# Queries and keys of layer 1's third head from seven products of quarters, in a two-layer hybrid step

## The chip, the core and the metric

The kernel runs on one core of one Trainium2 chip, in one launch. The metric is the device time of an execution in microseconds (us), lower is better; the time of a version is the median of its runs. One further execution is taken with the hardware profiler; all rows of the profile come from that one.

## The reference

Two layers over 640 token rows: one prompt of 512 rows and eight running streams of 16 rows each. Layer 0 is stick-breaking attention with 16 heads, layer 1 is gated linear attention (GLA) with 4 heads. What matters here is layer 1, cut to:

```python
q, k, v, r, a_lr = jnp.split(h @ w_in, [nk, 2 * nk, 2 * nk + nv, 2 * nk + 2 * nv], axis=-1)
# 4 heads: q and k 256 columns each, v and r 512 columns each; h has 2048 columns
g = log_sigmoid(a_lr @ w_a2 + b_a) / GLA_TAU           # the decays
S_t = diag(exp(g_t)) S_{t-1} + k_t^T v_t;  o_t = q_t S_t   # per head, in chunks
o = rmsnorm(o) * g_out
y = (o * silu(r)) @ w_out
```

The prompt starts from a zero state; each stream starts from its own state of 4 x 256 x 512 numbers, which is read and written once. All is float32 in and out.

## The kernel before

**Precision.** A float32 product is made of three matmuls in the type that TensorE runs at full rate: each operand is split into a high and a low half (`halves`, L134 on ScalarE and L135 on VectorE), and high x high, high x low and low x high are added up in PSUM.

**Two ways to project.** The activations of a layer are kept in quarters (`Quarters`: two halves of the 2048 columns, two halves of the 640 rows). `by_sevens` takes a job of 256 output columns and computes it with seven products of quarters in place of eight; the sums of quarters of the activations are ready (`sums`), those of the weights are made on VectorE for each job (L507 to L513). A product is 8 x 3 = 24 matmuls of 320 columns, a job 168 of them, all at L541. `plain` takes a part of 128 output columns and computes it directly: 2 x 2 x 8 x 3 = 96 matmuls of 320 columns at L596; two parts, 192 matmuls, stand for one job.

**Stages of layer 1.** First `six` and one call of `plain` make the first head's values and queries. Then a list `jobs` goes through `by_sevens` (L1352 to L1355), 17 jobs: keys of head 0, queries and keys of head 1, the values of heads 1 to 3 and the gates of all heads. Here nothing else is woven in but the short transposes that the values need. Then comes **the heads' stage** (from L1395 on), the GLA recurrence itself. Its PSUM banks are shared out anew, and its work is cut into lanes, each a generator:

- `decays` makes the decays of each head and scales its queries and keys;
- `prompt_lane` goes through 16 units (4 heads of 4 chunks of 128 rows). Each unit carries the state `S` on: scores, products with the state's two halves (`S1h`, `S1l`: one buffer each, L1582 and L1583), the update of `S` (L1646, L1648), then norm and transposes (L1470, L1474, L1492) and a store of the result `og`;
- `sample_lane` goes through 16 groups of 4 stream states. Per group: four matmuls at L1754 read four state tiles `s`, then four matmuls at L1760 and four operations at L1762 update them, and GpSimd's queue stores them and loads the next ones into the same buffers (7 buffers for 64 tiles). After a head's fourth group come norm, transposes and the store of its `og`;
- `fetches` reads the rows of `og` back, splits them and so prepares the output projection.

**Fillers.** The lanes are short instructions with waits between them. Between their steps, `drive` puts the long rows of matmuls that depend on no lane: first `others` (L1414), the plain products for queries and keys of heads 2 and 3 (8 parts, 768 matmuls at L596), and after them two calls of `share` (g = 0 and 1: 240 matmuls of 512 columns each at L642), which multiply the finished `og` rows of heads 0 and 1 by the output weights. `share` for g = 0 can start when both lanes are through head 0 and the rows of `og` are back; for g = 1 when head 1 is through. What is left of the output projection (L360 and L1894) follows when all lanes have ended.

**What sets the order.** TensorE's instructions are written in a fixed order, which it keeps: a step that isn't ready holds up all behind it. The place of each lane step is chosen at build time by a class `Side`: a clock `pe["now"]` is advanced by a cost per matmul that is issued, a lane says after how much of that clock its next step is due, and `tick` issues the steps that are due between two pieces of filler. Where no filler is left, the clock just goes on and the lane steps stand directly behind one another. The other engines' order is made by the tool's scheduler. The table `came` connects the filler with the lanes: `came["of"]` is the last head whose queries and keys have been made by `keep` (L1397), and `decays` does not start head 2 or 3 before that; `came["plain"]` and `came["last"]` let `fetches` use the buffers that the plain products share with it.

Of the kernel before, what the change touches and what calls it, by code (L numbers as in the profile page):

```python
# [15 lines left out]
P = 128  # L16
# [11 lines left out]
NK = 1024  # L28
# [13 lines left out]
def hybrid_step_kernel(ctx: ExitStack, tc: tile.TileContext, A: dict, O: list):  # L42
# [7 lines left out]
    pe = {"now": 0.0, "quad": 4800}  # L50
# [3 lines left out]
    def by(l, r):  # L54

        n = r.free_size()
        if l.dtype == F32R:
            pe["now"] += n / 2400 + 0.0133
        elif l.free_size() <= 32:
            pe["now"] += n / pe["quad"] + 0.01  # L60
        else:
            pe["now"] += n / 600 + 0.005
        return r
# [9 lines left out]
    def store(out, in_):  # L73
        nc.sync.dma_start(out=out, in_=in_)
# [24 lines left out]
    def bank(tag):  # L99
        return psum["pool"].tile([P, 512], F32, tag=tag, name=f"ps_{tag}", bufs=psum["bufs"][tag])  # L100
# [22 lines left out]
    gq_d, gk_d = ([dp.tile([P, 2, T], F32, name=f"{n}_{h}") for h in range(GH)] for n in ("gq", "gk"))  # L123
# [25 lines left out]
    def wraw(src, a, n):  # L149
        r = wp.tile([P, 1024], F32, tag="wr", name="wr", bufs=WR)[:, :a * n]  # L150
        load(r.rearrange("p (a n) -> p a n", a=a), src)
        return r

    def wsplit(r, a):
        return [t.rearrange("p (a n) -> p a n", a=a) for t in split(r)]
# [422 lines left out]
    def plain(h, src, parts, upper=None):  # L578

        todo = [(n0, k0, leave) for n0, leave in parts for k0 in (8, 0)]  # L580

        def piece(n):
            if n < len(todo):
                n0, k0, _ = todo[n]
                return wraw(src[:, k0 // 8:k0 // 8 + 15:2, n0:n0 + P], 8, P)

        nxt, raw, acc = wsplit(piece(0), 8), piece(1), None
        for n, (n0, k0, leave) in enumerate(todo):
            wh, wl = nxt
            if k0:  # L590
                acc = [bank("mm")[:, :HALF] for _ in hs]
            for nt in range(2):
                for k in range(8):
                    hi, lo = h.part(k0 + k, nt)
                    for l, r, first, last in ((wh, hi, True, False), (wh, lo, False, False), (wl, hi, False, True)):
                        mm(acc[nt], l[:, k, :], by(l[:, k, :], r), start=k0 == 8 and k == 0 and first,  # L596
                           stop=k0 == 0 and k == 7 and last)
                    if k % 2:
                        yield
                if nt == 0 and raw is not None:  # L600
                    nxt, raw = wsplit(raw, 8), piece(n + 2)
                if k0 == 0:
                    leave(nt, acc[nt])
            if upper is not None and n == len(todo) - 2:
                upper()

    def keep_in(d):
        def f(out):
            for hh in range(2):
                store(d[:, hh, :], out[hh])  # L610
        return f
# [77 lines left out]
    h1, h2 = Quarters(), Quarters()  # L689
# [8 lines left out]
    with tc.tile_pool(name="st", bufs=1, reuse_waits="tile") as st:  # L698
# [50 lines left out]
        def ring(tags):  # L749
            n = 0  # L750
            while True:
                tag = tags[n % len(tags)]
                yield ad_ring() if tag is None else sp.tile([P, 1024], F32, tag=tag, name="ar")
                n += 1
# [3 lines left out]
        last = ring(["s14", "s15", None, None])  # L758
# [38 lines left out]
    with tc.tile_pool(name="wq", bufs=1, reuse_waits="tile") as wq:  # L797
# [22 lines left out]
        def keep_value(p):  # L820
            return lambda out: side.add(rows0(out, p, v_d[p], vp_rows, vs_rows))

        jobs = []
# [328 lines left out]
    src = w_in1.rearrange("(kt p) n -> p kt n", p=P)  # L1152
    s1_pool = ExitStack()
    sp = s1_pool.enter_context(tc.tile_pool(name="sp1", bufs=1, reuse_waits="tile"))
    with tc.tile_pool(name="o0", bufs=1, reuse_waits="tile") as po, ExitStack() as only_d:
# [193 lines left out]
                    store(gr_d[h][:, kt, :], out[s])  # L1349
            return leave  # L1350

        jobs = [(NK, keep_in(gk_d[0])), (256, keep_in(gq_d[1])), (NK + 256, keep_in(gk_d[1]))]  # L1352
        jobs += [(2 * NK + 512 * h + 256 * n, keep_value(h, n)) for h in range(1, GH) for n in range(2)]
        jobs += [(2 * NK + D + 512 * h + 256 * n, keep_gate(h, n)) for h in range(GH) for n in range(2)]
        sevens = by_sevens(h2, w_in1, wq, jobs)  # L1355
# [37 lines left out]
        return w_out1.rearrange("(kt p) n -> p kt n", p=P)[:, k0:k0 + 2, 512 * c:512 * c + 512]  # L1393

    with tc.tile_pool(name="gl", bufs=1, reuse_waits="tile") as gl:  # L1395
        came = {"plain": False, "last": False, "of": 1, "when": 0.0}

        def keep(dst, hh):
            t = []

            def leave(nt, pt):
                if nt == 0:
                    t.append(gl.tile([P, T], F32, tag="pl", name="pl", bufs=2))
                    came["last"] = dst is gk_d[3] and hh == 1
                nc.scalar.copy(t[0][:, hs[nt]], pt)
                if nt:
                    nc.scalar.dma_start(out=dst[:, hh, :], in_=t[0])
                    for h in (2, 3):
                        if hh and dst is gk_d[h]:
                            came.update(of=h, when=pe["now"])  # L1410
            return leave


        others = plain(h2, src, [(n0 + P * hh, keep(dst, hh)) for h in (2, 3)  # L1414
                                 for n0, dst in ((256 * h, gq_d[h]), (NK + 256 * h, gk_d[h])) for hh in range(2)],
                       lambda: came.update(plain=True))
        for _ in range(2):
            next(others)
# [69 lines left out]
        def leave(h, t0, on, g):  # L1488

            tp = bank("tp")  # L1490
            for s in range(4):
                turn_block(tp[:, P * s:P * s + P], block(on[:, P * s:P * s + P]), ident)  # L1492
            dve.tensor_tensor(g, tp.rearrange("p (s t) -> p s t", s=4), g, op=ALU.mult)
            move(og_d[h][:, :, t0:t0 + P], g)
# [332 lines left out]
    with tc.tile_pool(name="o1", bufs=1, reuse_waits="tile") as po:  # L1827
# [54 lines left out]
        for i in range(4):  # L1882
            r = wraw(w_of(2 + i // 2, 3, i % 2), 2, 512)
            h, lo = (po.tile([P, 1024], F32R, name=f"{n}{i}") for n in ("kh", "kl"))
# [3 lines left out]
        for a in range(TOK):  # L1888
            acc = bank("mm")
            for n in range(8):  # L1890
                wh, wl = kept[n // 2]
                h, lo = (x[:, P * a:P * a + P] for x in og1[8 + n])
# [30 lines left out]
```

## Time and profile before

| what | before |
|---|---|
| median of 3 runs | 2579.01 us (2577.28 to 2580.81) |
| the profiled execution's own time | 2576.39 us |
| its span, first to last instruction | 2574.6 us |
| mean clock granted to TensorE | 0.979 of full speed |
| TensorE busy | 2444.2 us, 95% of the span |
| VectorE, ScalarE, GpSimd busy | 1604.6, 1019.7 and 231.4 us |
| moved by DMA | 502.05 MB, mean 195 GB/s |

The span is the distance between the first and the last instruction that the profiler saw; the execution's own time lies 1.8 us above it. The busy time of TensorE counts matmuls that overlap once. In the views below, rows of a timeline begin with start and length in us; an idle time in brackets is that of the engine just before the row, with what ended it. In a view by windows, each row is a stretch of the span, with the busy time of TensorE (PE), its weight loads (PEld), VectorE (DVE), ScalarE (ACT) and GpSimd (POOL) in it, the number of instructions in brackets, the granted clock (1.00 is full speed), the share of the 16 DMA engines in use and what they moved.

### The profile page before, as it was taken

How to read it: one execution, taken by the hardware profiler on the slowest of the kernel's cores; microseconds unless marked ns; L12 is line 12 of the kernel's file. 1: busy time of each engine (PE TensorE's matmuls, PEld its weight loads, DVE VectorE, ACT ScalarE, POOL GpSimd, SP SyncE). 2: the span in 40 equal slices, each digit the busy share in tenths (PEclk: the TensorE clock that was granted, in tenths of full speed). 3: DMA queues.
4: the chain of work that ended last, by engine and by line, in shares of the span. 5: the costliest groups of instructions: out<-in, count | busy, mean ns of one | idle time of the engine just before them, and what ended most of it. 6: DMA issues, size and time to landing. Idle time of an engine off the chain costs nothing. (4 is left out here: it accounts for less than half of the span.)

```text
span 2574.6 us, 43617 instructions
## 1 busy us (share of the span) xinstructions
PE 2444.2 (95%) x17321; PEld 2147.2 (83%) x17321; DVE 1604.6 (62%) x2445; ACT 1019.7 (40%) x1820; POOL 231.4 (9%) x489
## 2 busy tenths in 40 slices
PE   6899999999999999999999979899999998989998
PEld 4589999989999988787777758899999997766776
DVE  4675655555566656666776665766666655666466
ACT  4342222222223335655443344333333364565133
POOL 1220000000000000000000050000000114334200
PEclk8899999999999999999999989999999999999999
DMA  9966666766663366666665853344444367777464
GB/s 337 320 212 218 217 204 219 228 216 192 207 199 118 116 209 207 228 213 222 214 226 170 252 188 123 88 114 130 126 124 118 112 221 249 240 250 230 164 230 148
DMA packets 452797, 502.05 MB, mean 195 GB/s; under 512 B 26090, under 2 KB 349810, under 8 KB 452466
## 3 DMA queue, kind: packets, MB, share of 16 engines
q1 hardware_dynamic: 433090, 442.11, 54.1%
q0 software_dynamic: 16048, 51.92, 6.0%
q10 hardware_dynamic: 3456, 5.24, 0.6%
q8 instruction: 136, 2.23, 0.4%
q14 instruction: 67, 0.55, 0.1%
HBM read 410.05 MB, written 89.13 MB: 194 GB/s over the span
## 5 line engine op out<-in xcount | busy, mean ns | idle before, releaser
L541 PE MATMUL ps_mm<-sums,wh 128*128 128x320 f32 x2880 | 644.0, 312 | 2.2 <-ACT wh L134 2.2
L541 PEld LDWEIGHTS ps_mm<-sums,wh 128*128 128x128 f32 x2880 | 481.2, 189 | 11.3 <-issue 7.4
L541 PE MATMUL ps_mm<-h,wh 128*128 128x320 f32 x2160 | 484.7, 312 | 5.7 <-DVE u L547 3.2
L541 PE MATMUL ps_mm<-sums,wl 128*128 128x320 f32 x1440 | 446.4, 310 | 1.5 <-DVE wl L135 1.5
L541 PEld LDWEIGHTS ps_mm<-h,wh 128*128 128x128 f32 x2160 | 360.3, 188 | 22.1 <-issue 14.5
L135 DVE TENSOR_TENSOR wl<-wr,wh 128x1024 fp32r<-128x1024 f32 x192 | 236.0, 1230 | 213.9 <-ACT wh L134 213.1
L134 ACT CAST wh<-wb 128x1024 fp32r<-128x1024 f32 x178 | 186.8, 1049 | 449.6 <-PE ps_mm L541 381.6
L541 PE MATMUL ps_mm<-h,wl 128*128 128x320 f32 x1080 | 334.5, 310 | 0.7 <-DVE wl L135 0.7
L134 ACT CAST wh<-wr 128x1024 fp32r<-128x1024 f32 x192 | 201.6, 1050 | 316.0 <-PE ps_mm L541 194.1
L541 PEld LDWEIGHTS ps_mm<-sums,wl 128*128 128x128 f32 x1440 | 271.6, 189 | 2.0 <-DVE wl L135 2.0
L135 DVE TENSOR_TENSOR wl<-wb,wh 128x1024 fp32r<-128x1024 f32 x178 | 217.6, 1222 | 63.0 <-ACT wh L134 62.5
L642 PE MATMUL ps_mm<-wh,ogh 128*128 128x512 f32 x460 | 201.8, 439 | 13.2 <-ACT ogh L134 7.5
L596 PE MATMUL ps_mm<-h,wh 128*128 128x320 f32 x896 | 208.0, 319 | 6.1 <-ACT wh L134 3.3
L541 PEld LDWEIGHTS ps_mm<-h,wl 128*128 128x128 f32 x1080 | 203.5, 188 | 1.0 <-DVE wl L135 1.0
L642 PE MATMUL ps_mm<-wh,ogl 128*128 128x512 f32 x460 | 182.8, 397 | 0.6 <-DVE ogl L135 0.4
L642 PE MATMUL ps_mm<-wl,ogh 128*128 128x512 f32 x460 | 182.1, 396 | 0.0
L596 PEld LDWEIGHTS ps_mm<-h,wh 128*128 128x128 f32 x896 | 151.1, 191 | 17.6 <-issue 7.0
L596 PE MATMUL ps_mm<-h,wl 128*128 128x320 f32 x448 | 139.9, 312 | 3.1 <-DVE wl L135 3.1
L642 PEld LDWEIGHTS ps_mm<-wh,ogh 128*128 128x128 f32 x460 | 87.9, 191 | 41.5 <-issue 14.8
L898 DVE TENSOR_TENSOR_SCAN k<-k,zero_c 128x544 f32<-128x544 f32 (+4 forms) x96 | 93.3, 976 | 29.6 <-ACT k L894 16.9
L470 PE MATMUL ps_mm<-wh,h 128*128 128x512 f32 x288 | 101.7, 418 | 6.8 <-ACT h L134 4.9
L642 PEld LDWEIGHTS ps_mm<-wh,ogl 128*128 128x128 f32 x460 | 87.4, 190 | 21.8 <-DVE ogl L135 1.8
(341 smaller groups left out, 3830.6 us busy)
## 6 DMA issues: line engine op xcount, KB each, us to landing
ar<-in_w_ada_dram SPq DMA_DIRECT2D x160, 512.0 KB
wb<-in_sb_w_in_dram SPq DMA_DIRECT2D x82, 512.0 KB
kc<-in_cache_sb_k_dram SPq DMA_DIRECT2D x64, 512.0 KB
vc<-in_cache_sb_v_dram SPq DMA_DIRECT2D x64, 512.0 KB
wb<-in_gla_w_in_dram SPq DMA_DIRECT2D x51, 512.0 KB
wr<-in_gla_w_in_dram SPq DMA_DIRECT2D x45, 512.0 KB
wr<-in_sb_w_in_dram SPq DMA_DIRECT2D x44, 512.0 KB
ar<-in_w_ada_dram SPq DMA_DIRECT2D x64, 256.0 KB
```

Of the source, the lines that this page charges most:

```text
L134: nc.scalar.copy(hi, x)
L135: dve.tensor_tensor(lo, x, hi.bitcast(F32), op=ALU.subtract)
L470: mm(acc[a], l, by(l, r[:, e, :]), start=j == 0 and e == 0 and first, stop=j == 7 and e == 1 and last)
L541: mm(acc, l[:, k, :], by(l[:, k, :], r), start=start and k == 0 and first, stop=k == 7 and last, skip_group_check=True)
L596: mm(acc[nt], l[:, k, :], by(l[:, k, :], r), start=k0 == 8 and k == 0 and first, stop=k0 == 0 and k == 7 and last)
L642: mm(acc, l, by(l, r[:, e, :]), start=i == 0 and e == 0 and first, stop=i == 1 and e == 1 and last)
L898: dve.tensor_tensor_scan(kr, kr, zeros[:, :w], 1.0, ALU.mult, ALU.add)
```

## The change

The queries and keys of head 2 (the third) become two more jobs of `by_sevens`, behind those of head 1 and ahead of the values, and their four parts leave the plain products of the heads' stage. The list has 19 jobs then, and `others` has 4 parts (384 matmuls). `came["of"]` starts at 2, since head 2's queries and keys are there when the stage begins.

```diff
-        jobs = [(NK, keep_in(gk_d[0])), (256, keep_in(gq_d[1])), (NK + 256, keep_in(gk_d[1]))]
+        jobs = [(NK, keep_in(gk_d[0]))]
+        jobs += [(n0 + 256 * h, keep_in(d[h])) for h in (1, 2) for n0, d in ((0, gq_d), (NK, gk_d))]
...
-        came = {"plain": False, "last": False, "of": 1, "when": 0.0}
+        came = {"plain": False, "last": False, "of": 2, "when": 0.0}
...
-                    for h in (2, 3):
-                        if hh and dst is gk_d[h]:
-                            came.update(of=h, when=pe["now"])
+                    if hh and dst is gk_d[3]:
+                        came.update(of=3, when=pe["now"])
...
-        others = plain(h2, src, [(n0 + P * hh, keep(dst, hh)) for h in (2, 3)
-                                 for n0, dst in ((256 * h, gq_d[h]), (NK + 256 * h, gk_d[h])) for hh in range(2)],
+        others = plain(h2, src, [(n0 + P * hh, keep(dst, hh)) for n0, dst in ((256 * 3, gq_d[3]), (NK + 256 * 3, gk_d[3]))
+                                 for hh in range(2)],
                        lambda: came.update(plain=True))
```

With half the filler, the places of the lanes' steps on TensorE move. Two places show it.

The first is TensorE in the heads' stage, behind the last group of head 0's stream states (`s` in L1754 is a state tile, `qz` the queries, `krh` and `krl` the halves of the prompt's keys, `aTh` and `aTl` those of its scores, `on` a normed result that is transposed). Before:

```order
L596 MATMUL ps_mm<-h,wh 128x320 x2
L596 MATMUL ps_mm<-h,wl 128x320
L1445 MATMUL ps_tp<-v,aTh 128x512 x2
L1445 MATMUL ps_tp<-v,aTl 128x512
L1760 MATMUL ps_tp<-vst,kst_21143 128x512
```

The change, from the last state of the same group on:

```order
L1754 MATMUL ps_z<-s_22618,qz_21591 32x512
L1492 MATMUL ps_tp<-ident,on 128x128 x4
L1760 MATMUL ps_tp<-vst,kst_21593 128x512
L1445 MATMUL ps_tp<-v,krh 128x512 x2
L1445 MATMUL ps_tp<-v,krl 128x512
L1760 MATMUL ps_tp<-vst,kst_21593 128x512 x3
L1457 MATMUL ps_tp<-q,k 128x128 x2
L1605 MATMUL ps_tp<-ident,k 128x128 x2
L1445 MATMUL ps_tp<-v,aTh 128x512 x2
```

The rows of L596 between the lanes' steps are gone; in the change none stands from shortly behind the third group of head 0 on, and the first row of L642 comes only when head 0 is through both lanes and its rows are back.

The second place is the end of the stage, TensorE around the last group of stream states (head 3), with the last `share` (L642) and the first rows of the final projection (L360). Before:

```order
L1754 MATMUL ps_z<-s_24695,qz_21141 32x512
L1754 MATMUL ps_z<-s_24761,qz_21141 32x512
L642 MATMUL ps_mm<-wh,ogh 128x512
L642 MATMUL ps_mm<-wl,ogh 128x512
L642 MATMUL ps_mm<-wh,ogl 128x512
L1760 MATMUL ps_tp<-vst,kst_21143 128x512
```

The change:

```order
L1754 MATMUL ps_z<-s_24762,qz_21590 32x512
L1760 MATMUL ps_tp<-vst,kst_21592 128x512 x4
L1754 MATMUL ps_z<-s_24764,qz_21591 32x512
L1754 MATMUL ps_z<-s_24766,qz_21591 32x512
L1754 MATMUL ps_z<-s_24768,qz_21591 32x512
L1754 MATMUL ps_z<-s_24788,qz_21591 32x512
L1760 MATMUL ps_tp<-vst,kst_21593 128x512 x4
L1492 MATMUL ps_tp<-ident,on 128x128 x4
L360 MATMUL ps_mm<-wh,ogh 128x512
```

Before, 13 triples of L642 stand between the last two groups and 5 behind the last one; in the change the last `share` has ended ahead of them, and the lanes' steps follow one another.

## The prediction

> **What bounds the kernel now.** The page first, for who is busy:
>
> ```profile
> span 2574.6 us, 43617 instructions
> ...
> PE 2444.2 (95%) x17321; PEld 2147.2 (83%) x17321; DVE 1604.6 (62%) x2445; ACT 1019.7 (40%) x1820; POOL 231.4 (9%) x489
> ```
>
> TensorE is busy 95% of the span, so a matmul less should be time less. That average hides two different stages, so I then read the chain that ended last, in order of time (start, us, what):
>
> ```profile
> 1878.81 179.76 PE ps_mm L541 x1224
> ...
> 2305.13 5.05 DMA og_in<-og
> ...
> 2322.85 6.28 PE ps_mm L642 x27
> ...
> 2461.00 75.74 PE ps_mm L360 x328
> ```
>
> In the seven-products stage the chain is one solid run of L541: 179.76 / 1224 = 0.147 us per matmul, a job of 168 is 24.7 us. L642 goes at 6.28 / 27 = 0.233 us. Between them the chain hops from engine to engine. A busy window of the first stage:
>
> ```profile
> 1650.00:1675.40 25.40, 25.40 (x176) 25.40 (x175) 15.96 (x17) 8.76 (x10) 0.00 (x0) 1.00 0.40 109
> ```
>
> About one job: PE never idle at full clock, VectorE busy 16.0 of 25.4 us, ScalarE 8.8, DMA at 40%. TensorE is the bound there, and nothing else is near it.
>
> The heads' stage I read by its state groups. PE's timeline gives where it begins, the groups of L1754, the first L642 and the end:
>
> ```profile
> 2059.23 0.53 PE L596 MATMUL ps_mm<-h,wh 128*128 128x320 f32 x2 [0.68 <-DVE out L547]
> ...
> 2119.44 1.07 PE L1754 MATMUL ps_z<-s,qz 128*32 128x512 f32 x8
> ...
> 2133.98 1.06 PE L1754 MATMUL ps_z<-s,qz 128*32 128x512 f32 x8
> ...
> 2171.45 1.92 PE L1754 MATMUL ps_z<-s,qz 128*32 128x512 f32 x2 [6.54 <-DMA s<-in_state_gla_dram]
> ...
> 2259.98 0.48 PE L642 MATMUL ps_mm<-wh,ogh 128*128 128x512 f32 x1
> ...
> 2265.82 0.50 PE L642 MATMUL ps_mm<-wh,ogh 128*128 128x512 f32 x1 [2.85 <-ACT ogh L134]
> ...
> 2269.86 0.80 PE L642 MATMUL ps_mm<-wh,ogh 128*128 128x512 f32 x1 [2.39 <-ACT ogh L134]
> ...
> 2443.77 1.07 PE L1754 MATMUL ps_z<-s,qz 128*32 128x512 f32 x8
> ...
> 2452.03 0.50 PE L360 MATMUL ps_mm<-wh,ogh 128*128 128x512 f32 x1 [2.22 <-DVE gate L1493]
> ```
>
> I cut the stage, 2059.2 to 2452.0, at group starts: the first group of head 0; its third; its fourth; the first and fourth of head 1, of head 2, of head 3; the end.
>
> ```profile
> 2059.20:2119.40 60.20, 58.00 (x383) 56.02 (x383) 32.54 (x62) 37.95 (x72) 8.73 (x17) 1.00 0.71 227
> 2119.40:2151.60 32.20, 31.63 (x193) 26.82 (x192) 27.91 (x51) 22.70 (x44) 10.85 (x19) 1.00 0.78 253
> 2151.60:2163.90 12.30, 12.30 (x88) 11.09 (x90) 7.03 (x14) 4.38 (x9) 5.75 (x10) 1.00 0.85 287
> 2163.90:2223.00 59.10, 48.73 (x263) 41.74 (x262) 28.81 (x53) 30.90 (x60) 19.41 (x32) 0.88 0.69 206
> 2223.00:2276.50 53.50, 45.03 (x248) 35.27 (x247) 32.72 (x61) 25.00 (x51) 20.71 (x34) 0.94 0.83 285
> 2276.50:2317.90 41.40, 37.31 (x177) 28.33 (x176) 25.22 (x41) 29.00 (x52) 15.14 (x25) 1.00 0.71 221
> 2317.90:2360.50 42.60, 42.60 (x214) 32.49 (x214) 29.11 (x55) 25.00 (x50) 16.13 (x29) 1.00 0.66 221
> 2360.50:2404.10 43.60, 36.85 (x151) 28.02 (x150) 21.64 (x36) 13.64 (x26) 14.82 (x25) 0.88 0.64 199
> 2404.10:2443.80 39.70, 39.10 (x183) 28.62 (x183) 20.25 (x28) 4.03 (x5) 11.41 (x21) 1.00 0.54 179
> 2443.80:2452.00 8.20, 6.01 (x32) 4.11 (x31) 5.83 (x10) 3.37 (x5) 2.78 (x5) 1.00 0.37 121
> sum 392.80, PE 357.57 PEld 292.51 DVE 231.06 ACT 195.97 POOL 125.72; mean PE 35.76 PEld 29.25 DVE 23.11 ACT 19.60 POOL 12.57
> ```
>
> PE is idle 35 us of the 392.8, and its clock drops to 0.88 where it waits, although 768 + 480 matmuls of filler lie between the lanes' steps. So the lanes already hold TensorE up here; filler hides their waits and is not simply work in the way. That is the point of the whole forecast.
>
> **The change part by part.**
>
> *The two jobs added.* 2 x 168 = 336 matmuls at L541 by 0.147: **+49.4 us**, all on the path, since that stage is solid PE. Each job's weight sums, splits and evacuations hide under PE, by the window above; without that cover they'd be 16 us of VectorE each. The four stores go out on SP like those of the jobs before, at 40% DMA. Bounds: 49.3 to 51, the upper end for a short wait per job.
>
> *The four parts removed.* 384 matmuls at L596 by 0.147 = 56.4 us of PE work, with eight weight loads of 512 KB, eight splits, eight evacuations and four stores. If PE had nothing else to wait for, this would all come back, and 56.4 - 49.4 = 7 us would be gained. How much of it comes back is the question, and depends on what the lanes need with less filler. Their fixed costs:
>
> ```profile
> out_dram<-s POOLq DMA_DIRECT2D x64, 256.0 KB, 3.6
> s<-in_state_gla_dram POOLq DMA_DIRECT2D x62, 256.0 KB, 4.8
> ...
> og<-gate POOLq DMA_DIRECT2D x20, 256.0 KB, 3.9
> ```
>
> ```profile
> L1762 DVE SCALAR_TENSOR_TENSOR s<-s,es,ps_tp 128x512 f32<-128x512 f32 x64 | 46.7, 743 | 19.1 <-PE ps_tp L1760 18.4 <-DMA s<-in_state_gla_dram 0.2
> ...
> L78 POOL DMA_DIRECT2D out_dram<-s x64 | 35.2, 551 | 96.8 <-DVE s L1762 63.5 <-DVE on_ms L232 26.6 <-issue 2.3
> ...
> L1583 DVE SCALAR_TENSOR_TENSOR S1l<-S,e,S1h 128x512 fp32r<-128x512 f32 x24 | 17.9, 747 | 15.4 <-ACT S1h L1582 15.3
> ...
> L1582 ACT ACTIVATE S1h<-S,e 128x512 fp32r<-128x512 f32 x24 | 17.3, 720 | 17.2 <-PE ps_tp L1445 17.1
> ...
> L1474 ACT ACTIVATE on<-ps_tp,on_r 128x512 f32<-128x512 f32 x16 | 11.0, 686 | 15.4 <-POOL on_r L234 15.4
> ...
> L135 DVE TENSOR_TENSOR ogl<-og_in,ogh 128x640 fp32r<-128x640 f32 x10 | 8.1, 822 | 11.4 <-ACT ogh L134 11.4
> ```
>
> A state cycle, from one group to the next that needs its buffers: L1754 1.1, L1760 0.4, L1762 0.74, store 0.55 + 3.6, load 0.55 + 4.8 (GpSimd's 551 ns to issue, then the time to landing): 11.8 us. With 7 buffers, the fourth state of each group waits for the group before. By stretch, with the rows of filler counted in the order before and after:
>
> - To the first group of head 0: the same 330 matmuls ahead, 60.2, no gain.
> - To the third group: 54 matmuls fewer, 7.9 us of work. From the second group to the third it took 2151.6 - 2134.0 = 17.6 us; the cycle allows 12 to 14: I take **-4**.
> - Third to fourth group: no filler left. Before, the fourth state landed 2171.45 - 2151.6 = 19.9 us on; the cycle alone is 12, with four updates and GpSimd's queue behind them 14: **-6**.
> - Fourth group of head 0 to the first of head 1: before, 2171.45 to 2223.0, 51.6 us, with 156 matmuls of filler; in the change only 12 of L642, at the end. PE work falls to 19 us, and the chain sets the time: norm and transposes of head 0 about 5 (the last stretch's 8.2 us less its 15 rows of L642, 3.5), held up by two units of the prompt lane that stand ahead, each 2 x (0.72 + 0.75 + 0.7) = 4.3 us for the two halves of its state, its `og` out 0.7 + 3.9, its rows back 5.05 and split in two operations of 0.8; sum 25. Then `share` waits once more for the second pair of rows, before 2269.86 - 2259.98 = 9.9 us. Together 35 to 36: **-15.5**.
> - To the fourth group of head 1: 114 matmuls of L596 go and 84 more of L642 come (+2.8 us of work), while the wait for rows of the `share` (2.85 + 2.39 and a slow clock behind it, out of 8.5 us idle in this stretch) has moved ahead; I let 8 us go: **-5.5**.
> - Two stretches through head 2: 96 rows of L642 in place of 108 in each, work -2.8 each, of which the lanes' chain keeps a part: **-4** together.
> - On to head 3: 108 rows in place of 90, 4.2 us of work, half of it in idle time that is there already (6.8 us): **+2**.
> - Head 3's groups: 63 in place of 138, work -17.3; three state cycles of 11.8 are the floor, 35 of 39.7: **-5**.
> - The end: 15 rows of L642 go behind the last group, but norm, gate and transposes still stand ahead of L360: **-0.5**.
>
> Sum -38.5. Against it stands the clock:
>
> ```profile
> 2170.00:2175.00 5.00, 3.54 (x8) 1.88 (x9) 0.20 (x1) 0.00 (x0) 1.07 (x2) 0.50 0.55 202
> ...
> 2180.00:2190.00 10.00, 10.00 (x65) 9.38 (x64) 5.64 (x10) 5.68 (x12) 6.70 (x12) 1.00 0.75 193
> ...
> 2266.00:2272.00 6.00, 3.48 (x8) 2.00 (x9) 1.65 (x3) 1.86 (x3) 3.02 (x5) 0.54 1.00 381
> ```
>
> Behind the wait of 6.54 us the granted clock is 0.50, ten us later 1.00 again; behind two waits of 2 to 3 us it is 0.54. In the change the piece without filler (some 40 us, PE busy less than half) and the last groups would run so, and the first matmuls behind each. Some 8 us of matmuls at half clock that lie on the chain cost 4 us more: **+4**. Bounds 0 and 8.
>
> The Trainium skill, "TensorE: Matmul & The Clock Gate", section "HAM oscillation — how this bites in real kernels", says that a TensorE idle for over about 3.4 us falls back to half its clock and needs as long of sustained work to get it back. It speaks against this change, which takes filler from a stage with waits. The row of 0.50 agrees. By that page, four such restarts at half of 3.4 us each are an estimate of 7 us where I took 4, and the total would come out 3 us later.
>
> So the heads' stage shrinks by 38.5 - 4 = 34.5 us, and the kernel gets 49.4 - 34.5 = **15 us slower**. `decays` for head 2 loses its wait for `came["of"]`; it is then held only until both lanes are through head 0, which came later anyway.
>
> Against the profiled execution (2576.39, span 2574.6, 1.8 around it) this is 2591.4. The median of the runs shown, 2579.01, is 2.6 above that execution; the forecast for the median is 2579 + 15 = **2594**.
>
> **The rivals.**
>
> *The lanes have slack, and TensorE's work alone counts.* Then the filler's 56.4 us come back in full, the jobs cost 49.4, and the time is 2579 - 7 = 2572. For it: 357.6 of 392.8 us busy, and stretches such as 2317.9 to 2360.5 without any idle. Against: after the fourth group of head 0 there is nothing to put in place of the filler; for PE to stay full, the rows of `og` would have to be back 19 us after that group, and the chain above has 25 ahead of its first product. It decides if the stage without filler lasts under 20 us. This is the rival on the faster side.
>
> *The lanes set the pace throughout.* Then only the stretches up to head 0's fourth group (-10) and the last groups (-5) give anything, and the stretch between head 0 and head 1 takes as long as before: -15, so +34, 2613. For it: the stretch to head 3 takes 43.6 us with 36.9 busy, that to head 1 59.1 with 48.7, each with many short waits for ScalarE, VectorE and GpSimd. Against: the last group's end went through in 8.2 us although 15 rows of L642 lay in it, so the lanes can be quick where they must.
>
> *It comes out even.* Gain and cost within 0.2%, 5 us, which is about what a measurement of this kernel can tell from no change. It needs 10 to 20 us more than the 34.5 allowed, so an `og` that is back 10 us sooner than the chain says.
>
> That the change doesn't do what it says I rule out: the order shows both sides, 336 matmuls more and 384 fewer.
>
> **How the numbers follow.** Forecast (+5 to +25) 0.50, time 2594. Lanes at their own pace (+25 to +40) 0.18. Even 0.15. PE alone (-5 and below) 0.17. So slower 0.68, same 0.15, faster 0.17. Eight in ten: below, the rival at 2572 with 3 us for waits of before that may go; above, the rival at 2613 with 3 more of the clock's bound: 2569 to 2616.
>
> **What would show it.** Right: the heads' stage begins 49 us later; its first L642 comes near 128 us after that instead of 200.8 (2259.98 - 2059.23), with much idle PE and a clock under 0.8 in the 40 us before it; the last two groups about 10 us apart with little PE work; the heads' stage near 358 us. Wrong: a stage of 336 us with PE as busy as before (then the lanes had slack), or one of 376 and more, with PE waiting at every head.

## The result, and the profile after

| what | before | after |
|---|---|---|
| median of 4 runs | 2578.15 us (2576.88 to 2580.81) | 2606.56 us (2601.06 to 2609.93) |
| ratio to before | 1 | 1.0107, 95% interval 1.0093 to 1.0121 |
| span of the profiled execution | 2574.6 us | 2604.4 us |
| mean clock granted | 0.979 | 0.973 |

The change makes the kernel 28.4 us slower. The forecast was 15 slower. (One execution of a version further down, of 8353 us, is left out of its ratio.) The page of the changed kernel answers to the first lines shown of before:

```profile
span 2604.4 us, 43543 instructions
...
PE 2451.6 (94%) x17273; PEld 2147.8 (82%) x17273; DVE 1626.0 (62%) x2469; ACT 1025.4 (39%) x1822; POOL 229.3 (9%) x489
```

TensorE has 48 matmuls fewer and 7.4 us more busy time, in a span that is 29.8 us longer. That says that something has come to stand idle, not where. The timeline of TensorE after the change gives the marks by which the heads' stage is cut (start, length, instruction, and in brackets the idle time ahead of it with what ended it):

```profile
2110.51 0.53 PE L596 MATMUL ps_mm<-h,wh 128*128 128x320 f32 x2 [0.68 <-DVE out L547]
...
2174.76 1.06 PE L1754 MATMUL ps_z<-s,qz 128*32 128x512 f32 x8
...
2220.04 1.91 PE L1754 MATMUL ps_z<-s,qz 128*32 128x512 f32 x2 [6.93 <-DMA s<-in_state_gla_dram]
...
2246.65 0.73 PE L642 MATMUL ps_mm<-wh,ogh 128*128 128x512 f32 x1
...
2256.47 0.79 PE L642 MATMUL ps_mm<-wh,ogh 128*128 128x512 f32 x1 [6.07 <-ACT ogh L134]
...
2328.84 1.12 PE L1492 MATMUL ps_tp<-ident,on 128*128 128x128 f32 x4 [6.69 <-ACT on L1474]
...
2367.51 0.80 PE L1457 MATMUL ps_tp<-q,k 128*128 128x128 f32 x2 [4.68 <-DVE k L1555]
...
2460.66 0.40 PE L642 MATMUL ps_mm<-wh,ogl 128*128 128x512 f32 x1
...
2473.66 1.92 PE L1754 MATMUL ps_z<-s,qz 128*32 128x512 f32 x2 [2.88 <-DMA s<-in_state_gla_dram]
...
2481.29 0.80 PE L360 MATMUL ps_mm<-wh,ogh 128*128 128x512 f32 x1 [0.79 <-DVE gate L1493]
```

The stage begins at 2110.5 and no longer at 2059.2: the two jobs cost 51.3 us. It lasts 370.8 us and no longer 392.8: 22.0 came back. What follows it takes 123.1 us in place of 122.6. So 51.3 - 22.0 + 0.5 = 29.8, the whole difference of the spans.

Where those 22.0 come from is read from one view, the busy time by windows, with the stage cut in two at its first L642. Before:

```profile
2059.20:2260.00 200.80, 184.56 (x1130) 163.12 (x1130) 121.33 (x224) 113.80 (x220) 58.95 (x102) 0.97 0.75 240
2260.00:2452.00 192.00, 173.01 (x782) 129.40 (x779) 109.73 (x185) 82.16 (x149) 66.78 (x114) 0.96 0.65 208
```

After:

```profile
2110.50:2246.60 136.10, 111.23 (x632) 91.67 (x633) 88.45 (x167) 85.02 (x167) 41.55 (x73) 0.94 0.76 247
2246.60:2481.30 234.70, 199.78 (x895) 145.82 (x893) 135.67 (x236) 100.59 (x188) 84.40 (x143) 0.93 0.66 214
```

TensorE's busy time (the first number behind the length) falls from 357.6 to 311.0, by 46.6. Its idle time, length less busy, rises from 16.2 + 19.0 = 35.2 to 24.9 + 34.9 = 59.8, by 24.6. The difference is the 22.0. More of the new idle time lies behind the first L642, where filler stands until 2461, than in the piece that lost it, where I looked for it: the piece ahead is 64.7 us shorter, and the piece behind is 42.7 us longer.

The same stretches as in the prediction (to the first group of head 0; its third group; its last state; the first and fourth group of heads 1 and 2; the first of head 3; its last state; the end):

```profile
2110.50:2174.80 64.30, 58.98 (x387) 55.99 (x390) 35.09 (x64) 39.55 (x75) 9.02 (x17) 1.00 0.72 229
2174.80:2204.90 30.10, 26.86 (x148) 20.40 (x150) 27.16 (x51) 21.67 (x43) 11.32 (x19) 0.94 0.83 283
2204.90:2220.00 15.10, 6.97 (x31) 2.88 (x30) 6.00 (x14) 4.55 (x11) 9.52 (x16) 0.88 0.79 282
2220.00:2261.40 41.40, 27.13 (x103) 18.78 (x103) 30.51 (x57) 29.57 (x59) 15.23 (x25) 0.79 0.72 230
2261.40:2307.70 46.30, 44.47 (x220) 33.40 (x219) 24.92 (x50) 20.34 (x41) 19.23 (x33) 1.00 0.71 237
2307.70:2354.20 46.50, 37.69 (x165) 29.26 (x164) 23.76 (x40) 26.85 (x49) 16.56 (x26) 0.89 0.75 225
2354.20:2401.50 47.30, 42.62 (x198) 31.73 (x197) 33.80 (x63) 24.31 (x47) 14.89 (x26) 0.93 0.58 189
2401.50:2442.20 40.70, 36.05 (x170) 27.73 (x169) 23.20 (x38) 13.57 (x25) 16.04 (x27) 1.00 0.69 212
2442.20:2473.70 31.50, 25.20 (x111) 15.27 (x111) 16.14 (x23) 2.88 (x4) 11.42 (x21) 0.98 0.66 226
2473.70:2481.30 7.60, 5.00 (x11) 2.04 (x11) 3.54 (x7) 2.31 (x4) 2.74 (x5) 0.50 0.33 87
```

The third row and the fourth, but for 12 rows of L642 at its end, hold no filler: clock 0.88 and 0.79, TensorE busy 7 of 15 and 27 of 41 us. The last row of L596 stands at 2191.1, behind the second group of head 0 and ahead of its third, so 55 us go by without filler before the first L642. The sixth and seventh rows (from head 1's fourth group to head 2's first, and through head 2's groups; 46.5 and 47.3) took 41.4 and 42.6 before, the first with 4.1 us of idle time and the second with none. They had 109 and 108 rows of L642 where there are 96 now: less work, and each about 5 us longer. What TensorE waits for in the stage (us in total, times, the longest), by the view of the waits:

```profile
PE ps_z L1754 <- DMA s<-in_state_gla_dram: 15.2, 7, 6.9
PE ps_tp L1492 <- ACT on L1474: 14.4, 4, 6.7
PE ps_mm L642 <- ACT ogh L134: 6.1, 1, 6.1
PE ps_tp L1457 <- DVE k L1555: 4.7, 1, 4.7
```

The same two rows of before:

```profile
PE ps_z L1754 <- DMA s<-in_state_gla_dram: 7.9, 2, 6.5
...
PE ps_tp L1492 <- ACT on L1474: 3.6, 2, 2.3
```

The second wait is put down to ScalarE, but ScalarE waits itself. The timelines around it follow: of VectorE, which scales the sum of squares of the streams' result; of GpSimd, which raises that to the power -1/2; and of ScalarE, which scales the result by it:

```profile
2322.14 0.15 DVE L232 TENSOR_SCALAR on_ms<-oss 128x1 f32<-128x1 f32 x1
```

```profile
2323.32 0.74 POOL L78 DMA_DIRECT2D og<-gate  x1 [2.00 <-issue]
2326.26 0.56 POOL L78 DMA_DIRECT2D s<-in_state_gla_dram  x1 [2.19 <-issue]
2326.93 0.55 POOL L78 DMA_DIRECT2D out_dram<-s  x1
2327.50 0.57 POOL L234 TENSOR_TENSOR on_r<-on_ms,mhalf 128x1 f32<-128x1 f32 x1
```

```profile
2328.10 0.69 ACT L1474 ACTIVATE on<-ps_z,on_r 128x512 f32<-128x512 f32 x1 [6.05 <-POOL on_r L234]
```

The norm's factor `on_r`, 0.57 us of work on 128 numbers, could start at 2322.3 and starts at 2327.5: it stands in GpSimd's queue behind an `og` store, a state load and a state store, with idle times of 2.00 and 2.19 us ahead of the first two. ScalarE waits 6.05 us for it, and TensorE, whose next instruction is the transpose, 6.69.

### The profile page after: what moved, and what is told of

Same layout as the page of the kernel before. It is cut to its first block, busy times and chain, and to the rows that moved or that the text cites. A ratio compares the mean times of both kernels' runs of the same rounds, so it can differ in the third digit from the quotient of the medians.

```text
span 2604.4 us, 43543 instructions
## 1 busy us (share of the span) xinstructions
PE 2451.6 (94%) x17273; PEld 2147.8 (82%) x17273; DVE 1626.0 (62%) x2469; ACT 1025.4 (39%) x1822; POOL 229.3 (9%) x489
## 5 line engine op out<-in xcount | busy, mean ns | idle before, releaser
L541 PE MATMUL ps_mm<-sums,wh 128*128 128x320 f32 x3008 | 672.2, 312 | 2.7 <-ACT wh L134 2.7
L541 PEld LDWEIGHTS ps_mm<-sums,wh 128*128 128x128 f32 x3008 | 502.8, 188 | 11.8 <-issue 7.4
L541 PE MATMUL ps_mm<-h,wh 128*128 128x320 f32 x2256 | 505.6, 312 | 5.4 <-ACT wh L134 3.3
L541 PE MATMUL ps_mm<-sums,wl 128*128 128x320 f32 x1504 | 466.1, 310 | 1.5 <-DVE wl L135 1.5
L541 PEld LDWEIGHTS ps_mm<-h,wh 128*128 128x128 f32 x2256 | 376.5, 188 | 21.6 <-issue 14.4
L134 ACT CAST wh<-wb 128x1024 fp32r<-128x1024 f32 x186 | 195.2, 1049 | 464.1 <-PE ps_mm L541 399.3
L541 PE MATMUL ps_mm<-h,wl 128*128 128x320 f32 x1128 | 349.3, 310 | 0.5 <-DVE wl L135 0.5
L541 PEld LDWEIGHTS ps_mm<-sums,wl 128*128 128x128 f32 x1504 | 283.5, 188 | 2.0 <-DVE wl L135 2.0
L135 DVE TENSOR_TENSOR wl<-wb,wh 128x1024 fp32r<-128x1024 f32 x186 | 227.3, 1222 | 64.9 <-ACT wh L134 64.7
L642 PE MATMUL ps_mm<-wh,ogh 128*128 128x512 f32 x460 | 203.2, 442 | 12.3 <-ACT ogh L134 8.4
L541 PEld LDWEIGHTS ps_mm<-h,wl 128*128 128x128 f32 x1128 | 212.3, 188 | 0.9 <-DVE wl L135 0.9
L642 PE MATMUL ps_mm<-wh,ogl 128*128 128x512 f32 x460 | 182.9, 398 | 0.4 <-DVE ogl L135 0.4
L642 PE MATMUL ps_mm<-wl,ogh 128*128 128x512 f32 x460 | 182.7, 397 | 0.0
L596 PE MATMUL ps_mm<-h,wh 128*128 128x320 f32 x640 | 150.5, 322 | 8.5 <-ACT pl L1406 3.5
L642 PEld LDWEIGHTS ps_mm<-wh,ogh 128*128 128x128 f32 x460 | 88.5, 192 | 40.8 <-issue 14.8
L596 PEld LDWEIGHTS ps_mm<-h,wh 128*128 128x128 f32 x640 | 108.4, 193 | 14.1 <-ACT pl L1406 4.1
L898 DVE TENSOR_TENSOR_SCAN k<-k,zero_c 128x544 f32<-128x544 f32 (+4 forms) x96 | 93.2, 975 | 29.9 <-ACT k L894 17.2
L642 PEld LDWEIGHTS ps_mm<-wh,ogl 128*128 128x128 f32 x460 | 87.6, 191 | 21.4 <-DVE ogl L135 1.2
L596 PE MATMUL ps_mm<-h,wl 128*128 128x320 f32 x320 | 100.7, 315 | 2.1 <-DVE wl L135 2.1
```

Source lines behind the costliest of these rows:

```text
L134: nc.scalar.copy(hi, x)
L135: dve.tensor_tensor(lo, x, hi.bitcast(F32), op=ALU.subtract)
L541: mm(acc, l[:, k, :], by(l[:, k, :], r), start=start and k == 0 and first, stop=k == 7 and last, skip_group_check=True)
L642: mm(acc, l, by(l, r[:, e, :]), start=i == 0 and e == 0 and first, stop=i == 1 and e == 1 and last)
L898: dve.tensor_tensor_scan(kr, kr, zeros[:, :w], 1.0, ALU.mult, ALU.add)
```

## The experiments

My theory was that of the prediction: the plain products cover waits of the lanes, so to take them away gives back much less than their 56.4 us of work. The rivals: TensorE's work alone counts, and the lanes set the pace throughout. Ratios are each to runs of before on the same chip; 0.001 is 2.6 us. "Stage" is from its first to its first row of L360, by the profiled execution.

### Filler put back, with the two jobs kept

Idle plain parts go ahead of those of head 3; their results go to a spare place in memory (fill6 has two of them, fill8 four, fill10 six).

```diff
-        others = plain(h2, src, [(n0 + P * hh, keep(dst, hh)) for n0, dst in ((256 * 3, gq_d[3]), (NK + 256 * 3, gk_d[3]))
+        others = plain(h2, src, [(512 + P * i, dummy) for i in range(2)] +
+                       [(n0 + P * hh, keep(dst, hh)) for n0, dst in ((256 * 3, gq_d[3]), (NK + 256 * 3, gk_d[3]))
...
```

Two idle parts:

> The change with two idle parts of plain products put back ahead of head 3's, their result stored to a spare tensor (6 parts, 19 jobs); 192 matmuls more, 28.2 us of TensorE work. Theory 'filler covers waits': the heads' stage grows by much less than its work, some 8 to 10 us, time about 2616. Rival 'TensorE's work alone counts': +28, 2635. Rival 'the lanes set the pace': within 5 us of the change's 2607.

Four:

> The change with four idle parts put back (8 parts as before, 19 jobs); 56.4 us of TensorE work more. Theory 'filler covers waits': the heads' stage is back at about 393 us, +22, time about 2629, which is also before + 49.4 for the two jobs. Rival 'work alone': +56, 2663. Rival 'the lanes set the pace': 2607.

Six:

> The change with six idle parts (10 parts, 19 jobs). Theory 'filler covers waits': the more filler there is, the less is left to cover; the last two parts cost 15 to 25 of their 28.2 us, time about 2649. Rival 'work alone': 2691. Rival 'the lanes set the pace': 2607.

| parts in the stage | ratio | stage | idle before / behind the first L642 |
|---|---|---|---|
| 4 (the change) | 1.0107 [1.0093, 1.0121] | 370.8 | 24.9 / 34.9 |
| 6 (fill6) | 1.0217 [1.0202, 1.0232], 2631.56 us | 395 | 19.1 / 36.8 |
| 8 (fill8) | 1.0169 [1.0152, 1.0186], 2618.72 us | 386 | 18.6 / 12.8 |
| 10 (fill10) | 1.0315 [1.0298, 1.0332], 2655.25 us | 427 | 27.6 / 13.7 |

The windows of fill6:

```profile
2111.20:2266.20 155.00, 135.90 (x829) 120.80 (x830) 92.34 (x170) 88.50 (x172) 42.33 (x73) 0.96 0.74 237
2266.20:2506.20 240.00, 203.19 (x890) 146.99 (x888) 136.51 (x237) 102.76 (x190) 84.03 (x142) 0.91 0.64 208
```

and of fill8:

```profile
2106.20:2309.70 203.50, 184.94 (x1129) 162.72 (x1130) 124.25 (x228) 114.29 (x223) 61.34 (x103) 0.97 0.76 243
2309.70:2491.90 182.20, 169.38 (x783) 126.58 (x781) 108.47 (x182) 81.28 (x148) 65.11 (x112) 0.98 0.66 216
```

For the rival of work alone, four parts put back had to cost 56 us: fill8 costs 16 more than the change (0.0062), near the 22 of the theory. The single steps do not bear the theory out: the first two parts put back cost 28 us, their whole work of 28.2, as the rival had it (the theory: 8 to 10). The next two make the kernel 12 us *faster*. The last two cost 38 us (0.0146), more than their work, where I expected 15 to 25. A smooth "more filler, more covered" is wrong. The last column shows what changes: from 6 to 8 parts the idle time behind the first L642 falls from 36.8 to 12.8; from 8 to 10 that ahead of it grows from 18.6 to 27.6 (in fill10's longest execution, 2662.10). With 4 and 6 parts the `share` rows begin early and are spent about 20 us before the stage ends (the last at 2460.7 of 2481.3 in the change; at 2486.6 of 2506.2 in fill6); with 8 parts the last stands at 2490.0 of 2491.9. I read this as: what counts is which of the lanes' steps have filler beside them, and that moves with every change of the order. It is not shown by itself, since no run moves the same filler to other places.

### The removal without the jobs

Here head 2 reads head 1's queries and keys, and neither the jobs nor the parts that made its own are there.

```diff
-        jobs += [(n0 + 256 * h, keep_in(d[h])) for h in (1, 2) for n0, d in ((0, gq_d), (NK, gk_d))]
+        jobs += [(n0 + 256 * h, keep_in(d[h])) for h in (1,) for n0, d in ((0, gq_d), (NK, gk_d))]
...
-                load(q, gq_d[h])
-                load(k, gk_d[h])
+                load(q, gq_d[1 if h == 2 else h])
+                load(k, gk_d[1 if h == 2 else h])
```

> Neither the two jobs nor the four parts: head 2's queries and keys are left out, head 2 reads those of head 1 (17 jobs, 4 parts). The removal alone. Theory 'filler covers waits': before less 22 us, 2556, and the change less 49 to 51 for its two jobs. Rival 'work alone': before less 56, 2522. If the two added jobs also disturb the beginning of the heads' stage, which took 4 us longer in the change, 2552.

2553.60 us, 0.9912 [0.9896, 0.9928]: -22 us, with the stage in one row of the windows:

```profile
2055.50:2427.20 371.70, 314.86 (x1524) 238.07 (x1524) 222.16 (x401) 186.02 (x353) 125.92 (x215) 0.92 0.69 224
```

371.7 against the change's 370.8: the same stage. To take 56.4 us of matmuls away, with their loads, splits and stores, gives 22, without any job added; the rival's 2522 is 31 us off. The stretch to the first group of head 0 takes 61.2 us here, against 60.2 before and 64.3 in the change: some 3 us at the beginning of the stage go with the jobs, and the total of the stage doesn't show them. And the jobs cost what is left between the two kernels, 1.0107 - 0.9912 = 0.0195 or 50 us: the parts of the sum add up.

### The lanes alone

No plain products in the stage, and the `share` calls only when the lanes have ended; heads 2 and 3 read head 1's queries and keys.

```diff
-        others = plain(h2, src, [(n0 + P * hh, keep(dst, hh)) for n0, dst in ((256 * 3, gq_d[3]), (NK + 256 * 3, gk_d[3]))
...
-        drive(others)
+        side.until(lambda: min(through.values()) >= GH)
...
```

> The lanes of the heads' stage by themselves: no plain products in it at all (17 jobs; queries and keys of heads 2 and 3 are left out, both heads read those of head 1), and both calls of share only after the lanes have ended. The distance from the stage's first matmul to the first L642 is the lanes' own time. Theory 'filler covers waits': 290 to 320 us, against 130 us of TensorE work that the lanes hold, so that neither the lanes nor TensorE's work alone make the 371 us of the change. Rival 'the lanes set the pace': 350 us and more. Rival 'work alone': 200 to 240 us.

```profile
2057.00:2366.70 309.70, 175.40 (x661) 103.05 (x661) 178.01 (x353) 146.45 (x298) 126.09 (x217) 0.74 0.68 223
```

The lanes need 310 us by themselves (2605.15 us for the kernel, 1.0126 [1.0098, 1.0153]), with TensorE idle in 134 of them (33 in waits for normed results, 32 for states). So they don't set the pace throughout: the stage of the change is 61 us longer than they alone. Of the 310 us 134 are there for filler to lie in, and the change has 384 x 0.147 + 480 x 0.233 = 168 us of it: by the total every gap could be filled. That 59.8 us of idle time stay in the change must then have to do with where the filler stands, and where it can: `share` has to wait until head 0 is through.

### Half of the change

Only head 2's queries become a job; its keys stay two plain parts. All is computed.

```diff
-        jobs += [(n0 + 256 * h, keep_in(d[h])) for h in (1, 2) for n0, d in ((0, gq_d), (NK, gk_d))]
+        jobs += [(n0 + 256 * h, keep_in(d[h])) for h, n0, d in ((1, 0, gq_d), (1, NK, gk_d), (2, 0, gq_d))]
...
```

> Half of the change, nothing left out: only head 2's queries become a job, its keys stay with the plain products (18 jobs, 6 parts). By the run with 6 parts and 19 jobs, less one job of 24.7 us: 2607. If that run's stage of 395 us came only from its idle parts standing ahead of head 3's: halfway between the versions, 2591. Rival 'work alone': 2571.

2597.86 us, 1.0102 [1.0076, 1.0127]: half of the change costs as much as all of it. Its profiled execution is the longest of its four runs (2605.98); its windows there are

```profile
2091.40:2251.20 159.80, 139.52 (x829) 124.22 (x830) 91.03 (x167) 88.25 (x168) 45.73 (x76) 0.94 0.72 229
2251.20:2481.80 230.60, 199.76 (x889) 144.06 (x887) 137.71 (x239) 103.11 (x195) 80.93 (x139) 0.93 0.66 213
```

Its stage starts 32.2 us later than that of before, where one job is 25, so what is long in this execution lies ahead of the stage. The stage is 390 us, with real work in the six parts as in fill6 with idle ones (395): one job more (25 us) and nothing back for 28 us of matmuls less. The step from 6 to 8 parts is thus no artefact of the idle parts.

### What the lanes wait for: the state loads

57 of the 64 loads of states are left out: a group goes on with what its buffer holds. The stores stay. First in the changed kernel:

```diff
-                s0 = gl.tile([P, 512], F32, tag="s0", name="s0", bufs=S0)
-                move(s0, A["state_gla"][0, 2 * m + e, h, P * dt:P * dt + P, :])
+                n = len(held)
+                if n < S0:
+                    held.append(gl.tile([P, 512], F32, name=f"s0_{n}"))
+                    move(held[n], A["state_gla"][0, 2 * m + e, h, P * dt:P * dt + P, :])
+                s0 = held[n] if n < S0 else given.pop(0)
...
```

> The change without the reloading of state buffers: a group goes on with what its buffer holds, so 57 of the 64 loads of states are left out; the stores stay. TensorE waited 15 us for these loads in the change. If the state cycle is what the missing filler laid bare: 15 to 20 us less, 2589. If another wait stands right behind it (GpSimd's queue, the way of og): within 6 us of 2607.

2575.05 us, 1.0003 [0.9992, 1.0013]: -27 us against the change, more than the 15 to 20 that I expected.

```profile
2105.00:2240.40 135.40, 112.39 (x633) 93.78 (x633) 87.36 (x166) 85.06 (x166) 33.83 (x56) 0.92 0.70 225
2240.40:2449.00 208.60, 191.72 (x894) 144.00 (x892) 135.10 (x237) 101.90 (x190) 61.08 (x99) 0.96 0.56 183
```

The idle time behind the first L642 falls from 34.9 to 16.9; ahead of it nearly nothing changes (24.9 to 23.0), although the longest wait for a state, 6.93, stood there: other waits take its place. The waits for states are gone. Those for the norm are not; they were 15.3 us in the change (14.4 ahead of L1492 and 0.9 ahead of L1445) and are 17.2 here:

```profile
PE ps_tp L1492 <- ACT on L1474: 11.9, 3, 4.5
...
PE ps_tp L1457 <- ACT on L1474: 3.1, 1, 3.1
...
PE ps_tp L1445 <- ACT on L1474: 2.2, 1, 2.2
```

The same edit in the kernel before:

> The kernel before without the reloading of state buffers (57 of 64 loads of states left out, the stores stay). Theory 'filler covers waits': with 8 parts of filler most of the state cycle is hidden, so this gives 8 to 14 us against 27 in the change, ratio about 0.996. Rival 'the state cycle costs the same with any filler': 25 us and more, ratio 0.990, and then the missing filler laid bare something else.

2557.47 us, 0.9930 [0.9914, 0.9946]: -18 us, between the two expectations, so neither holds as it stands. The loads cost both kernels, the change 9 us more. Without them the change would still be 1.0003 / 0.9930 = 1.0073, or 19 us, slower than before: most of what did not come back is not theirs.

### Buffers, or the queue

`gate` and `vst`, two loads that stand in GpSimd's queue, go to SP's, in the changed kernel:

```diff
-            move(g, gr_d[h][:, :, t0:t0 + P])
+            load(g, gr_d[h][:, :, t0:t0 + P])
...
```

> The change with the loads of gates and of the stacked values moved from GpSimd's queue to SP's, so that the power of the norm (L234), which stands in the same queue as the states' loads and stores, waits for less. TensorE waited 14 us for normed results in the change, 6.7 us of it once. If the order in GpSimd's queue is the cause: 8 to 14 us less, 2596. If the loads only wait elsewhere: no change, or slower by up to 10 us, since SP's queue has waits of its own.

2596.77 us, 1.0091 [1.0071, 1.0111]: 4 us by the ratios, within the intervals, where 8 to 14 were expected if the order in the queue is the cause. Its waits in the stage:

```profile
PE ps_z L1754 <- DMA s<-in_state_gla_dram: 12.5, 5, 3.6
PE ps_mm L596 <- ACT wh L134: 5.5, 1, 5.5
...
PE ps_tp L1733 <- ACT on L1474: 3.9, 1, 3.9
...
PE ps_tp L1445 <- ACT on L1474: 2.7, 2, 2.2
PE ps_tp L1492 <- ACT on L1474: 2.4, 2, 1.8
```

The waits for the norm, all rows together, fell from 15.3 to 9.0, as they should if the queue held `on_r`; a wait for a split weight, 5.5, has come, whose load stands in the queue that took the two over. TensorE's idle time in the stage falls from 59.8 to 50.3.

Then 11 state buffers in place of 7 (room for them is made by giving up one pool of weights, w4), in the changed kernel:

```diff
-S0 = 7
+S0 = 11
...
-        with tc.tile_pool(name="w4", bufs=1, reuse_waits="tile") as w4:
-            ring3["pool"] = w4
+        if True:
```

> The change with 11 state buffers in place of 7, at the cost of the third pair of buffers for split weights in the share calls (pool w4), since there is no room for both. All is computed. If the state cycle is what the missing filler laid bare, as the run without reloading says (27 us): 15 to 25 us less than the change, ratio to before about 1.002. If the loads are late because the 16 DMA engines or GpSimd's queue are full and not because of buffers: within 5 us of the change, ratio 1.010.

2602.57 us, 1.0102 [1.0086, 1.0117]: no gain that can be told. By the waits the buffers did what they should:

```profile
PE ps_tp L1492 <- ACT on L1474: 24.0, 3, 14.9
PE ps_tp L1457 <- ACT on L1474: 6.3, 1, 6.3
...
PE ps_z L1754 <- DMA s<-in_state_gla_dram: 2.0, 1, 2.0
```

The waits for states went from 15.2 to 2.0, and those for the norm from 15.3 to 30.3; TensorE's idle time in the stage is 62.3. Four more loads are let into GpSimd's queue, and what stands behind comes later there: in the wait of 14.9 the norm's sum is ready at 2210.2 and `on_r` begins at 2222.2, behind an `og` store, three state loads, three state stores and six loads of `vst`. So my idea that buffers bound the time fell: with more of them the wait moves to other work in GpSimd's queue. What the loss of w4 cost in this run was not taken apart. In the kernel before, 11 buffers, and 11 buffers with `gate` and `vst` on SP:

> The kernel before with 11 state buffers in place of 7 and without pool w4. All is computed. TensorE waits 8 us for states there, with slow clock behind: 5 to 12 us less than before, ratio 0.997, if buffers are the cause; 1.000 if not, or up to 1.004 if the splits of the share weights now come late.

2571.72 us, 0.9981 [0.9968, 0.9994]: 5 us, the least that was expected from the buffers. State waits went from 7.9 to 3.0, those for the norm from 3.6 to 19.7.

> The kernel before with 11 state buffers, without pool w4, and with the loads of gates and of the stacked values on SP's queue and no longer GpSimd's. All is computed. With 11 buffers alone the waits for states fell from 8 to 3 us, but the waits for normed results, whose power is queued on GpSimd among the states' transfers, rose from 4 to 20. If GpSimd's queue is the common place: 6 to 12 us less than with the buffers alone, ratio to before about 0.994. If SP's queue only takes over the waits: 0.998 to 1.000.

2569.22 us, 0.9980 [0.9967, 0.9992], where 0.994 was expected if GpSimd's queue is the common place and 0.998 or more if SP's queue only takes over the waits. State waits are 0.2 and those for the norm 4.8, but others have come, 5.9 for a split weight and 5.6 for `S1h`: the idle time in the stage is 30.6, against 33.8 with the buffers alone and 35.2 before. These two are the only versions with all of the work that beat both kernels, by 0.2%, and can't be told from one another.

## Why the prediction was right in sign and short in size

It held that the filler in the heads' stage covers waits, so that 56.4 us of matmuls less give back much less than they cost elsewhere. The run without the jobs shows that by itself: -22 us for 56.4. The rival of TensorE's work alone is out by that run (31 us off) and by fill8. The lanes' pace throughout, as I had it, is out too: the stretch between heads 0 and 1 was to stay at 51.6 us and took 41.4, and the lanes alone need 310 of the 371. In size, though, +28.4 lies nearer to that rival's +34 than to the forecast's +15, in the band of +25 to +40. The stage of 370.8 us lies nearer to the 376 that was named as a sign of being wrong than to the 358 that was forecast.

In the profiled executions +29.8 stands against +15. Step by step:

- **The jobs**: 51.3 against 49.4, just above the bounds of 49.3 to 51: +1.9. What follows the stage adds 0.5.
- **To the first group of head 0**: 64.3 against 60.2: +4.1. I had called it equal since the same matmuls stand there; the waits for ScalarE in it grew. By the run without the jobs most of this goes with them.
- **To the third group, and to its last state**: -2.1 and -4.7 against -4 and -6: +1.9 and +1.3.
- **Between heads 0 and 1**: the times that I summed were met, the parts were not, so this hit is partly luck. The first L642 was to come 25 us behind the group's last state and came 2246.65 - 2220.04 = 26.6 behind it; the second pair of rows 9.9 later, and came 9.8 later. But the streams' gated result is there by 2230.8, and its store is issued at 2238.3 at the earliest, behind state stores and loads, `vst` and `gate` in GpSimd's queue, for which the sum had nothing. And the 6.07 us that TensorE waits for the second pair end with a split on ScalarE at 2255.7; ScalarE had stood idle 3.18 us for `on_r` until 2253.1, and had other work from there to the split. The 136.1 us from the start of the stage, against 128, come from the late steps ahead. Head 1's group does not stand right behind those rows: 41.4 us against 36, +5.3.
- **Head 1's groups**: -7.2 against -5.5: -1.7.
- **Head 2's two stretches**: +9.8 against -4: **+13.8, the step that failed.** I had counted less work there, and so less time. They had run with 4.1 us of idle time and with none before, and I took that for slack in the lanes; the likelier reading is that the filler just covered their waits. With 96 rows where there were 109 and 108, waits of 6.69 us (the norm behind GpSimd's queue) and 4.68 us (`k` from the decays) came out, and the clock fell to 0.89 and 0.93. That the missing rows alone let them out is argued: the order around them changed too.
- **On to head 3, its groups, the end**: -2.9, -8.2 and -0.6 against +2, -5 and -0.5: -8.2. Head 3's groups took 31.5 us, less than the 35 that I had called a floor of three state cycles: its third group starts 8.3 us behind the second, so a cycle of 11.8 us does not bound each step.
- **The clock** was a term of its own, +4, and is inside these stretches: -4.

The sum of the misses is 1.9 + 0.5 + 4.1 + 1.9 + 1.3 + 5.3 - 1.7 + 13.8 - 8.2 - 4 = 14.9 (in rounded numbers), all of the difference. That this is so near to head 2's 13.8 alone is chance: the other misses, +15.0 and -13.9, cancel.

The clock fell about as said: to 0.84 in the 40 us before the first L642, where I had said under 0.8, to 0.79 in the stretch between heads 0 and 1, and to 0.50 in the last 7.6 us, behind a wait of 2.88; in the lanes alone it is 0.74 over 310 us. The rule that the prediction takes from the Trainium skill, "TensorE: Matmul & The Clock Gate", section "HAM oscillation — how this bites in real kernels", agrees in kind with these rows, though the waits ahead of the row of 0.50, 1.60, 1.59 and 2.88 us, are each shorter than its 3.4. Whether its 7 us or my 4 was nearer no run here can tell, since none takes the clock's share apart from that of the waits. Busy time fell by 46.6 us where the rows removed are 56.4; the 9.8 between them go with the lower clock, but the views don't tell them from matmuls that overlap less.

Settled is that the removal gives 22 us, that the jobs cost 50, and that state loads cost the changed kernel 27 us. Open is how much of these 27 is the place in GpSimd's queue and how much the traffic itself, since the run without loads took both away, and which single wait makes 6 parts dearer than 8. To take `on_r` off GpSimd's queue was not tried.

## What to carry to other kernels

A stretch in which an engine hardly idles need not have slack: filler may be just enough there, and here a tenth less of it went with 10 us more. Before filler is taken from a stage with latency chains, run the chains alone (310 us here) and take the filler away alone (22 of 56 us came back): those two runs give the price that sums of busy time don't. More buffers for a transfer were worth little here, where its queue also carries the small operations that everybody waits for: the waits moved from 15.2 and 15.3 us to 2.0 and 30.3. That a wait got shorter is not yet time: what counts is the idle time of the stage, 59.8 against 62.3 there.

## What the runs showed of the hardware that was not expected

- A step of 0.57 us on GpSimd came 5.2 us late behind three DMA issues in the same queue, each 0.55 to 0.74 us long, with up to 2.2 us of idle time between; the profile shows the wait under ScalarE, 6.05, and TensorE, 6.69.
- In this kernel the same 56.4 us of matmuls were worth 16 to 22 us when all were taken and nothing for the first half of them (8 to 6 parts: 12 us slower with the idle parts, one job's 25 us unpaid with the real ones).
